# Fused trunk, MLP: scales behind the third product with tiles of their own, the first weight sums made ahead of the stage, two buffers for the values

## The chip, the cores and the metric

The kernel runs on one core of one Trainium2 chip. Its time is the device time of one execution in microseconds, the median of several runs. Below, the matrix engine is PE, the vector engine DVE, the scalar engine ACT, GpSimd POOL, and the engine that issues the transfers SP.

## The reference

Two layers over 1040 tokens (16 learned ones and 1024 given) of 1024 channels. Layer 0 mixes tokens with a short convolution and a gated delta rule, layer 1 with attention in a window. Each layer ends with an MLP whose gate goes through a causal convolution of width 3 along the tokens. All in float32. What the change touches is the MLP (w_up is 1024 x 5632, w_down 2816 x 1024):

```
for layer in range(DEPTH):
    hn = rms_norm(h, attn_norm_w[layer])
    ...
    h = h + mix.astype(h.dtype)
    ff = conv_ffn(rms_norm(h, ffn_norm_w[layer]), ffn_w_up[layer], ffn_conv_w[layer], ffn_w_down[layer])
    h = h + ff.astype(h.dtype)

def conv_ffn(h, w_up, conv_w, w_down):
    gate, val = jnp.split(h @ w_up, 2, -1)
    gate = causal_dwconv(gate, conv_w)
    return (jax.nn.silu(gate) * val) @ w_down
```

## The kernel before, in words

A float32 operand is kept as two rounded parts (tiles of the type that the profile calls fp32r), a high one and the low rest, and a product is three matmuls: high by high, high weights by low data, low weights by high data. High parts are made on ACT (a cast), low parts on DVE (a subtraction), in the stages' own weights at L134 and L135 (there on POOL or DVE), in the MLP at L814 and L815, for the MLP's data at L754 and L755.

The function ffn does an MLP. The tokens are cut in two halves of 520 columns (516 in layer 1), the channels into two halves of four tiles of 128. From these four blocks and the two halves of the weight columns it makes seven products instead of eight, in the manner of Strassen and Winograd: sums of data blocks on one side, sums of weight blocks on the other. The data side is made once for each MLP: X[0] to X[6], four tiles each, 28 tiles, with high and low parts. X[4] to X[6] are issued behind half_x, the last low part of X[3]. The weight side is made for each of the NF = 22 passes, each of 128 gate and 128 value columns.

A pass is seven products of 24 matmuls (L825), in this order: 0 into A (first, L842) and 1 into C, by the gate weights w1; 2 into A and 3 into C, by w2 (the sum sa = wv1 + wv2 - wg1 below and wv1 + wv2 above); 4 and 5 into A, by w3 (sb's first half, and wv2); 6 into C, by w4 (sb's second half). The first product of the next pass is put ahead of product 5. The buffers A and C are two banks each and rotate by two. ACT copies A out (p1, u2, u3); DVE adds to r (L871, L903) for the gate and to v (L894) for the values, multiplies the gate by the norm's factor (L904), does the convolution and the gate's nonlinearity (conv, L851 to L860), multiplies by v (L906), and SP writes the result to memory (fy, L907).

The norm's factor rstd isn't needed before L904, since it is taken out of the products. The function scales makes it from r, the sum of squares, which DVE adds up tile by tile (L741): four matmuls with ones (L761) for each half of tokens, and a short chain of ACT and DVE steps, in tiles th and sg which conv uses too.

Then comes the down projection: yf is read back from memory (L923), multiplied by rstd (L927), split into two parts (L928 on ACT, L929 on DVE), and multiplied by the down weights (gemm, L147), in five groups of passes (PARTS). Three loads of yf belong to the tail of the last pass, when PE still does its last products.

Tiles come from pools: fp is the MLP's own, wp is shared with the weights of the other stages (wo of the attention and the down weights too, through load_w). A tag in fp has one buffer if nothing else is said, in wp two; a writer waits for all readers of what was there before. In before, even passes load their weights into wp and odd ones into two buffers in fp; each third pair of high and low weight tiles is in fp, the others in wp. v has one buffer.

A scheduler sets the order of the instructions on each engine when the program is built, by the order in which the code issues them and when it thinks their operands are ready; a block under issue_after(x) comes behind x. That order is each engine's program. SP issues the transfers in its order too, and waits there for the buffers that they fill.

## Time and profile before

| what | value |
|---|---|
| median of 3 runs | 2385.93 us (2381.71 to 2390.98) |
| time of the profiled execution | 2385.68 us |
| its span | 2383.9 us |
| granted clock of PE, mean | 0.994 |
| PE busy | 2324.3 us, 98% |
| DVE busy | 1615.8 us, 68% |
| ACT busy | 973.4 us, 41% |
| POOL busy | 408.2 us, 17% |
| chain that ended last | PE 84%, DVE 10%, ACT 3% |

Times in rows are microseconds from the span's start. MLP 0 begins at about 583 and its passes end about 1041; MLP 1 begins at about 1668, when the attention's last product ends (1668.55), and its passes end about 2134. In a row of the timeline stand start, duration, engine, line, operation, result and operands, and the count; in square brackets the idle time of the engine before it and what ended that. Neighbouring rows of an engine can overlap by about 0.1 us, since an instruction begins while the one ahead drains: the step from one start to the next is the price of an instruction in a full queue.

### The profile page before, as it was taken

To read this page: it belongs to the slowest core of one execution; us is meant where nothing else is said; L and a number is where in the kernel's file an instruction comes from. 1 tells how busy PE (TensorE), PEld (TensorE's weight loads), DVE (VectorE), ACT (ScalarE), POOL (GpSimd) and SP (SyncE) were. 2 spreads that over 40 slices of the span, in tenths; PEclk is the share of its full clock that TensorE was granted. 3 is DMA by queue.
4 is the path that set the end of the run, shared out by engine and by line. 5 is a ranking of instruction groups with operands and counts; after the bars stand their busy time and mean duration, and the time that the engine had idled before them with its cause. 6 is when DMAs were issued, how large, how long until landed. Compare 5 with 4: busy or idle time off the path is not lost.

```text
span 2383.9 us, 39785 instructions
## 1 busy us (share of the span) xinstructions
PE 2324.3 (98%) x16000; PEld 2182.5 (92%) x16000; DVE 1615.8 (68%) x2799; ACT 973.4 (41%) x1952; POOL 408.2 (17%) x357
## 2 busy tenths in 40 slices
PE   8999999999999999999999999999899999999999
PEld 7989999999999999999999986778799999987887
DVE  8886745566877777777436466768977777778332
ACT  6544313434444444433116456656544444443110
POOL 1123323431000000012225233231000000002221
PEclk9999999999999999999999999999899999999999
DMA  4233534241222222154223110203222222234222
GB/s 139 79 128 121 170 111 138 76 161 72 89 81 81 81 76 76 63 188 139 66 60 129 45 36 19 89 27 116 81 89 81 81 81 77 72 142 169 76 67 102
DMA packets 93481, 224.83 MB, mean 94 GB/s; under 512 B 18672, under 2 KB 30264, under 8 KB 93296
## 3 DMA queue, kind: packets, MB, share of 16 engines
q1 hardware_dynamic: 93296, 222.28, 27.1%
q8 instruction: 126, 2.06, 0.3%
q14 instruction: 59, 0.48, 0.1%
HBM read 166.08 MB, written 56.15 MB: 93 GB/s over the span
## 4 chain that ended last, share of the span: by engine, by line
PE 84%; DVE 10%; ACT 3%; DMA 1%; issue 1%; POOL 0%; SPq 0%; ACTq 0%; DVEq 0%; POOLq 0%
PE mm L147 40%; PE A L825 20%; PE C L825 15%; PE scp L1067 1%; DVE qt L251 1%; PE po L1122 1%; DVE X L752 1%; PE qkp L971 1%; PE po L1125 1%; ACT xh L182 0%; DVE Xd L499 0%; DVE yl L171 0%; DVE fq L497 0%; DMA rb<-rq 0%; PE ptp L1096 0%
## 5 line engine op out<-in xcount | busy, mean ns | idle before, releaser
L825 PE MATMUL A<-X,whi 128*128 128x260 f32 (+1 forms) x2816 | 513.3, 283 | 5.6 <-ACT whi L814 3.2
L147 PE MATMUL mm<-y,wdh 128*128 128x346 f32 (+2 forms) x1760 | 471.0, 350 | 1.6 <-DVE r L903 1.6
L825 PEld LDWEIGHTS A<-X,whi 128*128 128x128 f32 x2816 | 434.0, 189 | 7.2 <-ACT whi L814 3.6
L825 PE MATMUL C<-X,whi 128*128 128x260 f32 (+1 forms) x2112 | 393.7, 285 | 7.8 <-DVE v L894 5.9
L825 PE MATMUL A<-X,wlo 128*128 128x260 f32 (+1 forms) x1408 | 392.6, 283 | 1.3 <-DVE wlo L815 1.3
L147 PEld LDWEIGHTS mm<-y,wdh 128*128 128x128 f32 x1760 | 315.1, 188 | 32.7 <-DVE r L903 2.0
L135 POOL TENSOR_TENSOR wdl<-wdr,wdh 128x512 fp32r<-128x512 f32 (+1 forms) x80 | 118.8, 1485 | 1311.7 <-ACT wdh L134 1302.4
L825 PEld LDWEIGHTS C<-X,whi 128*128 128x128 f32 x2112 | 330.7, 190 | 8.9 <-DVE v L894 6.3
L147 PE MATMUL mm<-y,wdl 128*128 128x346 f32 (+2 forms) x880 | 307.5, 350 | 0.6 <-POOL wdl L135 0.6
L825 PE MATMUL C<-X,wlo 128*128 128x260 f32 (+1 forms) x1056 | 297.5, 284 | 0.0
L825 PEld LDWEIGHTS A<-X,wlo 128*128 128x128 f32 x1408 | 264.2, 189 | 1.5 <-DVE wlo L815 1.5
L939 DVE TENSOR_TENSOR h<-mm,h 128x346 f32<-128x346 f32 (+2 forms) x200 | 115.9, 584 | 201.8 <-PE mm L147 201.0
L825 PEld LDWEIGHTS C<-X,wlo 128*128 128x128 f32 x1056 | 200.4, 190 | 0.0
L147 PEld LDWEIGHTS mm<-y,wdl 128*128 128x128 f32 x880 | 165.5, 188 | 16.8 <-POOL wdl L135 1.3
L815 DVE TENSOR_TENSOR wlo<-sa,whi 128x1024 fp32r<-128x1024 f32 x44 | 53.9, 1226 | 161.8 <-ACT whi L814 161.8
L134 ACT CAST wdh<-wdr 128x512 fp32r<-128x512 f32 (+1 forms) x80 | 53.1, 663 | 255.6 <-PE mm L147 221.9
L814 ACT CAST whi<-sb 128x512 fp32r<-128x512 f32 x88 | 54.7, 621 | 132.7 <-PE C L825 131.0
L147 PE MATMUL mm<-xl,wqkvh 128*128 128x346 f32 (+1 forms) x288 | 95.8, 333 | 1.4 <-DVE xl L183 1.4
L147 PE MATMUL mm<-xh,wqkvh 128*128 128x346 f32 (+1 forms) x288 | 96.3, 337 | 0.7 <-DVE row L269 0.7
L814 ACT CAST whi<-sa 128x1024 fp32r<-128x1024 f32 x44 | 46.1, 1048 | 115.7 <-PE A L825 115.0
L147 PE MATMUL mm<-xh,wqkvl 128*128 128x346 f32 (+1 forms) x288 | 93.0, 325 | 0.0
L928 ACT CAST y<-yf 128x346 fp32r<-128x346 f32 (+2 forms) x110 | 54.7, 536 | 93.1 <-DVE yf L927 73.7
(391 smaller groups left out, 5054.1 us busy)
## 6 DMA issues: line engine op xcount, KB each, us to landing
wg<-in_w_up SPq DMA_DIRECT2D x44, 512.0 KB, 3.2
wv<-in_w_up SPq DMA_DIRECT2D x44, 512.0 KB, 3.3
wdr<-in_w_down SPq DMA_DIRECT2D x48, 256.0 KB, 2.6
fy<-sg SPq DMA_DIRECT2D x22, 520.0 KB, 2.7
yf<-fy SPq DMA_DIRECT2D x22, 520.0 KB, 4.1
fy<-sg SPq DMA_DIRECT2D x22, 516.0 KB, 2.7
yf<-fy SPq DMA_DIRECT2D x22, 516.0 KB, 4.7
wdr<-in_w_down SPq DMA_DIRECT2D x32, 320.0 KB, 3.5
```

The lines of the kernel that those rows point to most:

```text
L134: ac.copy(hi, raw)
L135: eng.tensor_tensor(lo, raw, hi.bitcast(F32), ALU.subtract)
L147: pe.matmul(ps[:, :n], a[:, j, :], b[:, c0:c0 + n], start=(i == 0), stop=(i == last))
L251: ve.scalar_tensor_tensor(d, buf[:, pad + c0 - i:pad + c0 - i + n], taps[W - 1 - i], tmp[:, :n], ALU.mult, ALU.add)
L752: last_lo[:] = [ve.tensor_tensor(lo, src, hi.bitcast(F32), ALU.subtract).ins]
L814: ac.copy(hi, src)
L815: ve.tensor_tensor(lo, src, hi.bitcast(F32), ALU.subtract)
L825: pe.matmul(ps[:, b, :q], a[:, at + k, :], x[:, c], start=(start and n == 0), stop=(n == 11), skip_group_check=not start)
L928: ac.copy(yh[:, s], yf[:, s])
L939: ve.tensor_tensor(hn[m][:, s], ps[:, :n], hn[m][:, s], ALU.add)
L971: pe.matmul(p2[:, :n], ct[:, C_BD:C_BD + P], sq, start=True, stop=True)
L1067: pe.matmul(ps[:, :nk], qg[G][t][r, tok], kx[G][r, cols], start=True, stop=True)
```

## The change

Four things are changed, all in ffn; the arithmetic stays.

1. The scales are issued behind product 2 of pass 0, and no longer ahead of the passes. They take sg (half 0) or th (half 1) for their intermediate values, each half in its own, and the last step's tile t is rstd itself.
2. The weights of pass 0 are loaded, and its sums sa and sb and the two parts of sa made, ahead of the norm's squares (raws0, sa0, w20, sb0). For the other passes the same sums are made in the functions s21 and s34 as before.
3. v has two buffers. The temporaries t2 of the data side lie in these two (four halves), and no longer in two half tiles and v.
4. Which pool a tile comes from turns with the count of tiles: even passes now load into fp's two buffers, odd ones into wp, and of each three pairs of weight tiles the first is in fp.

```diff
@@ -724,9 +724,53 @@
                     def wide(tag):
                         return pu.tile([P, 2, 512], F32, tag=tag, name=tag)
 
-
                     def full(tag, bufs=1):
                         return fp.tile([P, 2 + 2 * hf], F32, tag=tag, name=tag, bufs=bufs)
+
+                    nw = [0]
+
+                    def wtile():
+                        nw[0] += 1
+                        p = fp if nw[0] % 3 == 1 else wp
+                        t = tuple(p.tile([P, KT, P], F32R, tag=tag, name=tag) for tag in ("whi", "wlo"))
+                        return t
+
+                    def wsplit(t, at, n, src):
+                        hi, lo = (x[:, at:at + n, :] for x in t)
+                        ac.copy(hi, src)
+                        ve.tensor_tensor(lo, src, hi.bitcast(F32), ALU.subtract)
+
+                    def weights(i):
+                        raws = []
+                        for n, at in (("wg", i), ("wv", NF + i)):
+                            r = (wp if i % 2 else fp).tile([P, KT, P], F32, tag="wraw", name=n, **({} if i % 2 else {"bufs": 2}))
+                            sp.dma_start(r, w_up[layer, at])
+                            raws.append(r)
+                        return raws
+
+                    def s21(raws):
+
+                        (wg, wv) = raws
+                        sa = fp.tile([P, KT, P], F32, tag="ws", name="sa", bufs=2)
+                        ve.tensor_tensor(sa[:, 4:8], wv[:, 0:4], wv[:, 4:8], ALU.add)
+                        ve.tensor_tensor(sa[:, 0:4], sa[:, 4:8], wg[:, 0:4], ALU.subtract)
+                        return sa
+
+                    def s34(raws, sa):
+
+                        (wg, wv) = raws
+                        sb = fp.tile([P, KT, P], F32, tag="ws", name="sb", bufs=2)
+                        ve.tensor_tensor(sb[:, 0:4], wg[:, 0:4], wv[:, 0:4], ALU.subtract)
+                        ve.tensor_tensor(sb[:, 4:8], sa[:, 0:4], wg[:, 4:8], ALU.subtract)
+                        return sb
+
+
+                    raws0 = weights(0)
+                    sa0 = s21(raws0)
+                    w20 = wtile()
+                    wsplit(w20, 0, KT, sa0)
+                    sb0 = s34(raws0, sa0)
+
 
                     sums = full("r", 2)
                     ss = [sums[:, s * hf:s * hf + hf] for s in range(2)]
@@ -759,15 +803,14 @@
                         ps = wide("C")
                         for b in range(2):
                             pe.matmul(ps[:, b, :q], ones, ss[s][:, b * q:b * q + q], start=True, stop=True)
-                        t = full("th")[:, :hf]
-                        ay = full("sg")
+                        ay, t = full("th" if s else "sg"), rstd[:, tk[s]]
                         a, y = ay[:, :hf], ay[:, hf:2 * hf]
                         ac.activation(two(a), ps[:, :, :q], AF.Identity, scale=1.0 / D, bias=epsc)
                         ac.activation(y, a.bitcast(I32), AF.Exp, scale=-0.5 * LN2 / (1 << 23), bias=seed)
                         for i, (sc, m3) in enumerate(((1.0, -3.00033), (0.25, -0.75))):
                             ac.activation(t, y, AF.Square, scale=sc)
                             ve.tensor_tensor(t, a, t, ALU.mult)
-                            ve.scalar_tensor_tensor(rstd[:, tk[s]] if i else y, t, m3, y, ALU.add, ALU.mult)
+                            ve.scalar_tensor_tensor(t if i else y, t, m3, y, ALU.add, ALU.mult)
 
                     w = [col(V_FN + 8 * layer + k) for k in range(KT)]
 
@@ -778,8 +821,8 @@
                         parts(1, k, B(1, k, 0), w[4 + k])
 
 
-                    vt2 = full("v")
-                    t2 = [half("t2", 2, "t2") if k < 2 else vt2[:, (k - 2) * hf:(k - 1) * hf] for k in range(4)]
+                    vt2 = [full("v", 2) for _ in range(2)]
+                    t2 = [vt2[k // 2][:, k % 2 * hf:(k % 2 + 1) * hf] for k in range(4)]
                     for k in range(4):
                         b11, b12, b21, b22 = B(0, k, 0), B(0, k, 1), B(1, k, 0), B(1, k, 1)
                         ac.activation(b12, b12, AF.Copy, scale=w[k])
@@ -790,8 +833,6 @@
                         parts(3, k, B(0, k, 0))
 
                     half_x = last_lo[0]
-                    for s in range(2):
-                        scales(s)
                     with tc.issue_after(half_x):
                         for k in range(4):
                             ve.scalar_tensor_tensor(B(0, k, 1), B(1, k, 1), w[4 + k], B(0, k, 1), ALU.mult, ALU.subtract)
@@ -800,19 +841,6 @@
                             ve.scalar_tensor_tensor(B(1, k, 0), B(1, k, 0), w[4 + k], t2[k], ALU.mult, ALU.subtract)
                             parts(5, k, B(1, k, 0))
                             parts(6, k, B(1, k, 1), w[4 + k])
-
-                    nw = [0]
-
-                    def wtile():
-                        nw[0] += 1
-                        p = fp if nw[0] % 3 == 0 else wp
-                        t = tuple(p.tile([P, KT, P], F32R, tag=tag, name=tag) for tag in ("whi", "wlo"))
-                        return t
-
-                    def wsplit(t, at, n, src):
-                        hi, lo = (x[:, at:at + n, :] for x in t)
-                        ac.copy(hi, src)
-                        ve.tensor_tensor(lo, src, hi.bitcast(F32), ALU.subtract)
 
                     def product(ps, wt, at, j, start):
                         hi, lo = wt
@@ -831,17 +859,9 @@
                         ac.copy(two(t), ps[:, :, :q])
                         return t
 
-                    def weights(i):
-                        raws = []
-                        for n, at in (("wg", i), ("wv", NF + i)):
-                            r = (fp if i % 2 else wp).tile([P, KT, P], F32, tag="wraw", name=n, **({"bufs": 2} if i % 2 else {}))
-                            sp.dma_start(r, w_up[layer, at])
-                            raws.append(r)
-                        return raws
-
                     def first(i):
 
-                        raws = weights(i)
+                        raws = weights(i) if i else raws0
                         w1 = wtile()
                         wsplit(w1, 0, KT, raws[0])
                         A = wide("A")
@@ -863,34 +883,35 @@
                     nxt = first(0)
                     for i in range(NF):
                         (wg, wv), w1, A, p1 = nxt
-                        g1, g2, v1, v2 = wg[:, 0:4], wg[:, 4:8], wv[:, 0:4], wv[:, 4:8]
+                        v2 = wv[:, 4:8]
                         Bk = wide("C")
                         product(Bk, w1, 4, 1, True)
                         r = full("r", 2)
                         ve.memset(r[:, 0:2], 0.0)
                         ve.tensor_tensor(two(r[:, 2:2 + hf]), Bk[:, :, :q], two(p1), ALU.add)
-
-                        sa = fp.tile([P, KT, P], F32, tag="ws", name="sa", bufs=2)
-                        w2 = wtile()
-                        with tc.issue_after(half_x) if i == 1 else nullcontext():
-                            ve.tensor_tensor(sa[:, 4:8], v1, v2, ALU.add)
-                            ve.tensor_tensor(sa[:, 0:4], sa[:, 4:8], g1, ALU.subtract)
-                            wsplit(w2, 0, KT, sa)
+                        if i == 0:
+                            sa, w2, sb = sa0, w20, sb0
+                        else:
+                            with tc.issue_after(half_x) if i == 1 else nullcontext():
+                                sa = s21((wg, wv))
+                                w2 = wtile()
+                                wsplit(w2, 0, KT, sa)
                         product(A, w2, 0, 2, False)
                         u2 = snap("u2", A)
+                        if i == 0:
+                            for s in range(2):
+                                scales(s)
                         C = wide("C")
                         product(C, w2, 4, 3, True)
-
-                        sb = fp.tile([P, KT, P], F32, tag="ws", name="sb", bufs=2)
                         w3 = wtile()
                         with tc.issue_after(half_x) if i < 2 else nullcontext():
-                            ve.tensor_tensor(sb[:, 0:4], g1, v1, ALU.subtract)
-                            ve.tensor_tensor(sb[:, 4:8], sa[:, 0:4], g2, ALU.subtract)
+                            if i:
+                                sb = s34((wg, wv), sa)
                             wsplit(w3, 0, 4, sb[:, 0:4])
                             wsplit(w3, 4, 4, v2)
                         product(A, w3, 0, 4, False)
                         u3 = snap("u3", A)
-                        v = full("v")
+                        v = full("v", 2)
                         ve.tensor_tensor(two(v[:, hf:2 * hf]), two(u3), C[:, :, :q], ALU.subtract)
                         if i + 1 < NF:
                             nxt = first(i + 1)
```

What the scheduler makes of it, at three places. First DVE in the tail of MLP 0's last pass, before:

```order
L927 TENSOR_TENSOR yf<-yf,rstd 128x348
L927 TENSOR_TENSOR yf<-yf,rstd 128x346 x2
L860 SCALAR_TENSOR_TENSOR sg<-th,sg 128x1040
L929 TENSOR_TENSOR y<-yf,y 128x348
L929 TENSOR_TENSOR y<-yf,y 128x346 x2
L906 TENSOR_TENSOR sg<-sg,v 128x1040
L894 TENSOR_TENSOR v<-u_10971,C 128x520
L903 TENSOR_TENSOR r<-u_10911,C 128x520
```

and after:

```order
L948 TENSOR_TENSOR yf<-yf,rstd 128x348
L948 TENSOR_TENSOR yf<-yf,rstd 128x346 x2
L915 TENSOR_TENSOR v<-u_10968,C 128x520
L880 SCALAR_TENSOR_TENSOR sg<-th,sg 128x1040
L950 TENSOR_TENSOR y<-yf,y 128x348
L950 TENSOR_TENSOR y<-yf,y 128x346 x2
L927 TENSOR_TENSOR sg<-sg,v 128x1040
L924 TENSOR_TENSOR r<-u_10908,C 128x520
```

The step that writes v (L894 before, L915 after; u is the copy u3, C the buffer of products) stood behind the multiplication by the old v (L906, now L927) and behind the low parts of y (L929, now L950); it now stands behind the steps on yf alone (L927, now L948). The order in MLP 1's tail is moved alike.

Second, SP at the same place, before:

```order
L131 DMA wdr<-in_w_down 128x512
L907 DMA fy_5957<-sg 128x1040
L923 DMA yf<-fy_5939 128x1040
L923 DMA yf<-fy_5940 128x1040
L923 DMA yf<-fy_5941 128x1040
L131 DMA wdr<-in_w_down 128x512
```

and after:

```order
L131 DMA wdr<-in_w_down 128x512
L928 DMA fy_5957<-sg 128x1040
L944 DMA yf<-fy_5939 128x1040
L944 DMA yf<-fy_5940 128x1040
L131 DMA wdr<-in_w_down 128x512
L944 DMA yf<-fy_5941 128x1040
L131 DMA wdr<-in_w_down 128x512
```

fy are the passes' results in memory, yf what the down projection reads of them, wdr the down weights, whose buffer in wp is one that the last pass's weights held. A load of down weights has moved ahead of the third load of yf.

Third, DVE at the end of the attention, ahead of MLP 1, before:

```order
L1188 TENSOR_TENSOR h_16829<-mm,h_16829 128x346
L741 TENSOR_TENSOR r<-r,sq 128x516
L1188 TENSOR_TENSOR h_16874<-mm,h_16874 128x334
L755 SCALAR_TENSOR_TENSOR X_17570<-h_16829,vt,X_17570 128x516
L755 SCALAR_TENSOR_TENSOR X_17573<-h_16116,vt,X_17573 128x516
L741 TENSOR_TENSOR r<-r,sq 128x516
L1188 TENSOR_TENSOR h_16874<-mm,h_16874 128x346
L135 TENSOR_TENSOR wol<-wor,woh 128x1024
```

and after:

```order
L755 TENSOR_TENSOR sa<-wv 128x512
L763 TENSOR_TENSOR sb<-wg,wv 128x512
L799 SCALAR_TENSOR_TENSOR X_17578<-h_16542,vt,X_17578 128x516
L785 TENSOR_TENSOR r<-r,sq 128x516
L1209 TENSOR_TENSOR h_16826<-mm,h_16826 128x334
L135 TENSOR_TENSOR wol<-wor,woh 128x1024
L756 TENSOR_TENSOR sa<-sa,wg 128x512
L799 SCALAR_TENSOR_TENSOR X_17590<-h_16587,vt,X_17590 128x516
L1209 TENSOR_TENSOR h_16826<-mm,h_16826 128x346
L785 TENSOR_TENSOR r<-r,sq 128x516
L764 TENSOR_TENSOR sb<-sa,wg 128x512
```

L1188 (now L1209) adds the attention's output products to h, L135 makes the low part of the output weights wo for one of these, L741 (now L785) adds squares, L755 (now L799) makes low parts of X. The two sums sa and sb of pass 0 (L755, L756, L763 and L764 after) now stand among these, and the low part of sa (L741 after) follows two rows further on; they stood behind the last of the L135 before. PE at this place had one half of the scales ahead of product 0 and the other behind it; now products 0 and 1 come first, and the scales' matmuls stand on both sides of the first matmuls of product 2.

## The prediction

> **What bounds the kernel now.** I read the page first, then PE's waits by what ended them, then windows over the passes and over the start of each MLP, then the single rows there. The page and the waits:
>
> ```profile
> span 2383.9 us, 39785 instructions
> PE 2324.3 (98%) x16000; PEld 2182.5 (92%) x16000; DVE 1615.8 (68%) x2799; ACT 973.4 (41%) x1952; POOL 408.2 (17%) x357
> ...
> engine line waited for: us in total, times, longest us
> PE C L761 <- DVE r L741: 8.9, 2, 7.9
> ...
> PE C L825 <- DVE v L894: 5.9, 2, 3.1
> ...
> PE A L825 <- ACT whi L814: 3.2, 2, 2.5
> ...
> PE C L825 <- DVE r L871: 1.4, 1, 1.4
> ```
>
> PE is busy for 2324.3 of 2383.9 us, so at most 59.6 us of its idle time can go. Three places that the diff touches hold 8.9 + 5.9 + 3.2 + 1.4 = 19.4 us of it: the matmuls of the scales (L761), product 6 behind the values (L894), and the first weights of each MLP. The windows (PE, PEld, DVE, ACT, POOL busy, PEclk, DMA share, GB/s), a steady stretch of passes first, then the start of MLP 0, then that of MLP 1:
>
> ```profile
> 650.00:670.00 20.00, 20.00 (x169) 20.00 (x168) 15.38 (x19) 8.55 (x12) 0.00 (x0) 1.00 0.22 80
> ...
> 585.00:595.00 10.00, 9.03 (x72) 8.70 (x71) 10.00 (x16) 8.37 (x15) 0.00 (x0) 1.00 0.14 56
> ...
> 1675.00:1680.00 5.00, 0.00 (x0) 0.00 (x0) 5.00 (x8) 3.91 (x8) 0.00 (x0) 0.50 0.00 0
> 1680.00:1685.00 5.00, 4.62 (x17) 4.25 (x18) 4.09 (x9) 4.28 (x8) 0.00 (x0) 0.50 0.00 0
> ```
>
> In the passes PE has no idle time and DVE works 15.38 of 20 us: an edit there gains nothing. At the starts it is the other way round: DVE is full and PE is the one with holes, at half clock behind the long one. So I take a start to be bounded by DVE's sum of work up to the last of the 28 X tiles, and a tail by the chain of DVE steps in front of product 6. That decides the forecast, because removing a wait of PE in front of a full DVE only moves the wait.
>
> **Start of MLP 1: -1.4 us.** The DVE rows that bound it, and PE's waits at both ends:
>
> ```profile
> 1666.51 1.23 DVE L815 TENSOR_TENSOR wlo<-wg,whi 128x1024 fp32r<-128x1024 f32 x1 [0.91 <-ACT whi L814]
> ...
> 1669.96 0.69 DVE L876 TENSOR_TENSOR sa<-wv 128x512 f32<-128x512 f32 x1
> 1670.56 0.75 DVE L787 SCALAR_TENSOR_TENSOR t<-h,vt,h 128x516 f32<-128x516 f32 x1
> ...
> 1682.51 0.69 DVE L770 SCALAR_TENSOR_TENSOR rstd<-th,sg 128x516 f32<-128x516 f32 x1 [0.91 <-DVE th L769]
> ...
> 1710.32 0.76 DVE L755 SCALAR_TENSOR_TENSOR X<-h,vt,X 128x516 fp32r<-128x516 f32 x1
> ...
> 1680.38 2.09 PE L761 MATMUL C<-r,ct 128*128 128x258 f32 x4 [7.93 <-DVE r L741]
> ...
> 1711.13 0.38 PE L825 MATMUL C<-X,whi 128*128 128x258 f32 x1 [0.53 <-DVE X L755]
> ```
>
> PE's last wait of the start is for X: product 6 of pass 0 begins its last k at 1711.13, behind DVE's step at 1710.32; from there PE is full. From the norm's first residual sum to that X step, DVE has 108 instructions in both orders, the same ones, only in another sequence. Their sum doesn't change, so the end can move only by DVE's idle time in between. That is 0.91 us at 1666.51 (the low part of pass 0's first weights waits for ACT's high part, and that for the weights' load) and 0.91 at 1682.51 (the scales' chain waits for its own last step): 1.8 us. The first goes since pass 0's weights now lie in the pool that is free early and their loads are issued first; the second goes since the scales stand later, among other work. What comes in is DVE waiting for the attention's output products: the moved weight sums stand in front of three of the low parts of wo (L135), for which those products wait. They are five steps, four of 128x512 at 0.60 (1669.96 to 1670.56) and one of 128x1024 at 1.14 (its duration of 1.23 less the 0.09 by which the row at 1669.96 overlaps the next), 3.55 us. PE will stall there for part of it; DVE has other work meanwhile. The trace has no such wait; the nearest rows are the two of 0.91, so I bound DVE's new idle time by 0 and 0.9 and take the middle, 0.4, since the steps in front are work that DVE must do anyway. -1.8 + 0.4 = -1.4, between -0.9 and -1.8. The 8.9 us in front of the scales vanish from the view of waits, and come back as waits for wo and X.
>
> **Start of MLP 0: -1.4 us.**
>
> ```profile
> 580.16 0.52 DVE L699 TENSOR_TENSOR h<-mm,h 128x346 f32<-128x346 f32 x1 [2.63 <-PE mm L147]
> ...
> 586.80 1.22 DVE L815 TENSOR_TENSOR wlo<-sa,whi 128x1024 fp32r<-128x1024 f32 x1
> ...
> 597.57 0.69 DVE L888 TENSOR_TENSOR sb<-sa,wg 128x512 f32<-128x512 f32 x1
> ...
> 614.08 0.77 DVE L755 SCALAR_TENSOR_TENSOR X<-h,vt,X 128x520 fp32r<-128x520 f32 x1
> ```
>
> Here DVE idles before 580 (2.63 us at 580.16) and is full from there on. The change puts the low part of the second weights (586.80, 1.14 us) and the two halves of sb (0.60 each; the second is the row at 597.57) into the idle stretch: -2.35 us. Two steps of the scales, now later in the order, fall in front of the last X step instead of behind it: 2 x 0.60 = +1.2. The last X step so ends 1.15 us earlier. Of what PE has left at that point, two matmuls fewer (0.12 us each) remain: -0.24. Sum -1.4; bounds -0.5 (X steps held by ACT's high parts) and -1.7. That PE now waits less at 598 (the 2.5 us of the view) gains nothing more, by the same reasoning.
>
> **The two tails: -3.2 and -4.4 us.** MLP 0's last pass, DVE, then PE; then MLP 1's:
>
> ```profile
> 1032.32 1.36 DVE L927 TENSOR_TENSOR yf<-yf,rstd 128x348 f32<-128x348 f32 x3
> 1033.61 1.23 DVE L860 SCALAR_TENSOR_TENSOR sg<-th,sg 128x1040 f32<-128x1040 f32 x1
> 1034.76 1.36 DVE L929 TENSOR_TENSOR y<-yf,y 128x348 fp32r<-128x348 f32 x3
> 1036.05 1.23 DVE L906 TENSOR_TENSOR sg<-sg,v 128x1040 f32<-128x1040 f32 x1
> 1037.38 0.70 DVE L894 TENSOR_TENSOR v<-u,C 128x520 f32<-128x520 f32 x1
> 1041.30 0.70 DVE L903 TENSOR_TENSOR r<-u,C 128x520 f32<-128x520 f32 x1 [3.22 <-PE C L825]
> ...
> 1034.74 0.28 PE L825 MATMUL A<-X,wlo 128*128 128x260 f32 x1
> 1038.13 0.51 PE L825 MATMUL C<-X,whi 128*128 128x260 f32 x2 [3.12 <-DVE v L894]
> ...
> 2128.75 0.69 DVE L894 TENSOR_TENSOR v<-u,C 128x516 f32<-128x516 f32 x1
> 2133.92 0.69 DVE L903 TENSOR_TENSOR r<-u,C 128x516 f32<-128x516 f32 x1 [4.48 <-PE C L825]
> ...
> 2126.46 0.28 PE L825 MATMUL A<-X,wlo 128*128 128x258 f32 x1
> 2129.49 0.80 PE L825 MATMUL C<-X,whi 128*128 128x258 f32 x2 [2.75 <-DVE v L894]
> ```
>
> Product 6 accumulates into C, which L894 must have read; L894 writes v, of which there is one buffer, so it stands behind the multiplication that reads the old v (L906). With two buffers it stands behind the yf steps alone: it can start at 1033.61 and end at 1034.31, before product 5's last matmul ends (1034.74 + 0.28 = 1035.02). So the 3.12 us go and product 6, 24 matmuls at 0.12 = 2.87 us, ends at 1037.9. Then DVE is next: the same five steps fill it to 1037.38 + 0.70 = 1038.08, so L903's step moves from 1041.30 to 1038.08: -3.2. MLP 1: product 5 ends at 2126.74, product 6 then at 2129.5 to 2129.6, DVE is free at 2129.45; L903's step moves from 2133.92 to 2129.55: -4.4. This is more than its wait of 2.75, since behind the wait the matmuls run slow (0.80 for two against 0.51 in MLP 0). Everything behind L903 (the down projection, full on PE) shifts with it.
>
> The Trainium skill (TensorE: Matmul & The Clock Gate, Part 1, The HAM clock gate) says that the clock falls to half after an idle window of about 3.4 us. By that rule alone a wait of 2.75 us would cost no clock, MLP 1's tail would give 2.9, and the sum would be 1.5 smaller; the rows show slow matmuls behind 2.75 us and nearly full ones behind 3.12, so the rows decide (the page's free-running window leaves room for this).
>
> **Sum.** -1.4 - 1.4 - 3.2 - 4.4 = -10.4 us. The profiled execution took 2385.68 us, of which the span is 2383.9; it becomes 2375.3. The median of the three runs, 2385.93, is 0.25 above it, so I forecast 2375.5. A measurement of this kernel tells about 0.5%, 11.9 us, from no change: the sum stays just within. If every term reaches its upper bound it is -1.7 - 1.8 - 3.2 - 4.4 = -11.1, still within.
>
> **Rivals.**
> 1. PE's waits are the limit after all: all 19.4 us of them go, with the half clock behind them (half of the 4.62 busy us in 1680 to 1685, 2.3, and the 1.5 of MLP 1's tail): up to 23.2 us. Against it: DVE's full windows. For it: PE may find other products ready in the new sequence, so that less is left behind the last X step. At 19.4 to 23.2 us: 2362.7 to 2366.5; it shares out down to 11.9 us, 1.5 more than my sum. Chance 0.27, half of it above 2367.
> 2. The tails don't come, because L894's place isn't what holds it, but the copy of u3 or the buffer C: only the starts, 2385.9 - 2.8 = 2383.1. Against it: DVE runs without a gap from 1032.32 to 1038.08, so its order does hold it. Chance 0.10, partial losses included.
> 3. Slower: the tail's third load of yf. In SP's order a load of down weights, which must wait until the last pass's gate and value weights are used (the low part of wv, DVE L815), now stands in front of it:
>
> ```profile
> 1015.45 7.50 SPq L923 DMA_DIRECT2D yf<-fy  x3
> 1025.67 0.69 DVE L815 TENSOR_TENSOR wlo<-wv,whi 128x512 fp32r<-128x512 f32 x1
> ...
> DMA to landing us min/median/max: 4.3/7.8/11.2
> ...
> yf<-fy SPq DMA_DIRECT2D x22, 520.0 KB, 4.1
> ```
>
> Before, the three were issued by 1022.9; now the third goes out at about 1026.6 (1025.67 + 0.69 and the issue). At the median of 4.1 it lands at 1030.7, in time for DVE's yf step at 1032.32. But the v step now stands behind that yf step, and the three steps behind it (1.15, 1.29, 1.33 by the starts above) in front of L903's. From a landing of 5.7 each us counts, from 9.0 MLP 0's tail gains nothing. The row with min, median and max is of the weights' loads (L838) between 470 and 620; at their longest, 11.2, yf lands at 1037.8, v is done at 1039.8, DVE is full to 1043.5, and L903's step is 2.2 late instead of 3.2 early. With 2.1 for MLP 1, worked out likewise, -2.8 + 4.3 = +1.5: 2387.4, slower than before from a landing of 10.4 on. Chance 0.03, since yf's own median is 4.1. The Trainium skill (DMA: Bandwidth & Descriptors, Issuing engines are not separate DMA queues) has transfers interleave on the same 16 engines whoever starts them; by that the weights in front would lengthen this landing. No run here shows the two together.
> 4. A wait in each pass: the tiles of high and low parts change places among the pools, and their ring could come round too early.
>
> ```profile
> 796.83 1.22 DVE L815 TENSOR_TENSOR wlo<-sa,whi 128x1024 fp32r<-128x1024 f32 x1 [4.03 <-ACT whi L814]
> ...
> 800.88 0.40 PE L825 MATMUL A<-X,whi 128*128 128x260 f32 x2
> ```
>
> The low part of a pass's second weights is done at 798.05, product 2 uses it from 800.88: 2.8 us to spare. It decides when a reused tile comes free 2.8 us later than now; a wait of 0.27 us in 44 passes would make 11.9, 2397.8. The ring has three pairs of tiles in the same rotation in both, so 0.04.
> 5. The second buffer isn't given and the sequence stays: the order shows the v step moved, so 0.01.
>
> My forecast has 0.55. Faster by over 0.5%: 0.27 (rival 1). Within: 0.55 + 0.10 + 0.03 + 0.01 = 0.69. Slower: 0.04 (rival 4). A range of 2367 to 2384 holds the forecast, rival 2 and half of rival 1: about 0.8.
>
> **What would show it.** Right: no wait of PE for v at either tail, L147 beginning 3.2 and 4.4 us sooner after product 5; the wait for the scales' sums gone, but waits for X of similar length in the 40 us after the attention; DVE full up to the last X step, which comes 1 to 2 us earlier. Wrong: DVE idle for over 2 us between 1642 and 1710, PE waiting for yf or wol for more than 3 us, or holes on PE in the steady passes.

## The result and the profile after

The changed kernel takes 2374.07 us (median of 6 runs, 2370.27 to 2378.61) where the kernel before takes 2387.45 (6 runs of the same session, 2381.71 to 2390.98): a ratio of 0.9946, with a 95% interval of 0.993 to 0.9962. That is 13.4 us less; the forecast was 10.4 less. The profiled execution has a span of 2368.5 us, 15.4 less than before.

From the page of the profile after, and from its view of PE's waits:

```profile
span 2368.5 us, 39717 instructions
PE 2320.9 (98%) x16000; PEld 2179.6 (92%) x16000; DVE 1607.0 (68%) x2799; ACT 973.2 (41%) x1952; POOL 412.8 (17%) x357
...
PE A L853 <- ACT u L859: 3.1, 4, 1.6
PE A L853 <- ACT p L859: 3.0, 1, 3.0
PE mm L147 <- DVE h L1209: 3.0, 4, 1.1
PE A L853 <- ACT whi L740: 2.8, 2, 1.9
...
PE A L853 <- DVE X L796: 2.3, 2, 1.7
```

The waits for r in front of the scales (8.9 us) and for v (5.9) are gone. In MLP 1's start, waits for ACT's copy p (3.0 us), for weights (whi, 2.8) and for X (2.3) stand in place of the one of 7.9 for r: PE idles 8.2 us there, before 10.8. At the end of the attention waits for h are new (3.0 us). The long hole in the windows of MLP 1's start has become several short ones (PE, PEld, DVE, ACT, POOL busy, PEclk, DMA share, GB/s; the same work comes about 10 us earlier than in the rows of before):

```profile
1665.00:1670.00 5.00, 3.27 (x24) 2.80 (x23) 4.17 (x7) 3.11 (x6) 0.00 (x0) 1.00 0.44 175
1670.00:1675.00 5.00, 3.71 (x16) 3.53 (x17) 4.96 (x9) 4.33 (x8) 0.00 (x0) 0.66 0.00 0
1675.00:1680.00 5.00, 4.65 (x40) 4.44 (x38) 5.00 (x9) 5.00 (x11) 0.00 (x0) 1.00 0.00 0
1680.00:1685.00 5.00, 1.37 (x7) 0.96 (x7) 5.00 (x10) 2.77 (x5) 0.00 (x0) 0.96 0.32 105
1685.00:1690.00 5.00, 4.74 (x22) 4.74 (x23) 5.00 (x9) 1.88 (x4) 0.00 (x0) 0.50 0.01 3
```

MLP 0's tail on the timeline after, DVE and then PE:

```profile
1026.34 1.37 DVE L948 TENSOR_TENSOR yf<-yf,rstd 128x348 f32<-128x348 f32 x3
1027.63 0.68 DVE L915 TENSOR_TENSOR v<-u,C 128x520 f32<-128x520 f32 x1
1028.24 1.23 DVE L880 SCALAR_TENSOR_TENSOR sg<-th,sg 128x1040 f32<-128x1040 f32 x1
...
1032.92 0.68 DVE L924 TENSOR_TENSOR r<-u,C 128x520 f32<-128x520 f32 x1
...
1028.74 0.29 PE L853 MATMUL A<-X,wlo 128*128 128x260 f32 x1
1028.86 0.41 PE L853 MATMUL C<-X,whi 128*128 128x260 f32 x2
...
1031.73 0.48 PE L147 MATMUL mm<-y,wdh 128*128 128x348 f32 x2
```

Product 6 follows product 5 at the next step (1028.74, 1028.86), because v is done at 1028.3. And the down projection begins at 1031.73, ahead of the r step at 1032.92: before, it began 0.75 us behind the start of that step.

To see where the time came from, I cut each execution at the same PE instructions: mixer (of which the stretch from its 941st to its 976th matmul, at 170 to 180 us, is shown alone), MLP start (from the last L147 matmul in front to the 481st matmul of the products), MLP tail (from the 3601st of these to the first L147 matmul of the down projection), and the attention's end (the last 260 matmuls or so of L147). Differences to the first profile of before, in us, from the starts of these instructions in each trace:

| stretch | after | after, again | before, again | second buffer alone | scales alone | sums alone |
|---|---|---|---|---|---|---|
| mixer, 170 to 180 | -3.8 | -2.4 | 0.0 | -0.2 | 0.0 | 0.0 |
| MLP 0 start | -1.0 | -1.0 | +1.2 | +0.2 | +1.8 | +0.8 |
| MLP 0 tail | -4.3 | -4.3 | +1.5 | -3.3 | +1.4 | -0.9 |
| attention's end | +3.4 | +3.5 | +0.2 | -0.2 | -0.2 | +3.4 |
| MLP 1 start | -2.8 | -3.8 | -0.2 | +0.6 | 0.0 | -3.6 |
| MLP 1 tail | -5.3 | -5.3 | +0.1 | -4.3 | +0.1 | +0.1 |
| whole span | -15.4 | -12.6 | +3.5 | -7.0 | +2.2 | +5.7 |

| stretch | all but second buffer | all but scales | all but sums | sums behind wo | squares on POOL | squares left out |
|---|---|---|---|---|---|---|
| mixer, 170 to 180 | 0.0 | -0.2 | 0.0 | -3.2 | -3.8 | 0.0 |
| MLP 0 start | +0.6 | +0.9 | +2.6 | +0.6 | +2.0 | +0.4 |
| MLP 0 tail | +0.6 | -2.4 | -4.3 | -4.3 | -4.3 | -4.3 |
| attention's end | +3.4 | +3.4 | -0.2 | +2.2 | +8.8 | +2.2 |
| MLP 1 start | -3.9 | -2.8 | +1.0 | -3.4 | -2.5 | -4.9 |
| MLP 1 tail | -2.3 | -4.3 | -5.2 | -5.3 | -5.3 | -5.3 |
| whole span | -2.6 | -5.9 | -8.7 | -14.4 | -3.1 | -10.8 |

The passes take the same time to 0.3 us in all. The rest of a span (the down projections, the other parts of mixer and attention) differs by up to 3.1 us in a stretch from the first profile of before, and by up to 1.2 us between the two of before.

### The profile page after: what moved, and what is told of

It is laid out like the page before. It is cut to its first block, busy times and chain, and to the rows that moved or that the text cites. A ratio compares the mean times of both kernels' runs of the same rounds, so it can differ in the third digit from the quotient of the medians.

```text
span 2368.5 us, 39717 instructions
## 1 busy us (share of the span) xinstructions
PE 2320.9 (98%) x16000; PEld 2179.6 (92%) x16000; DVE 1607.0 (68%) x2799; ACT 973.2 (41%) x1952; POOL 412.8 (17%) x357
## 4 chain that ended last, share of the span: by engine, by line
PE 85%; DVE 9%; ACT 3%; DMA 2%; issue 1%; POOL 1%; SPq 0%; ACTq 0%; DVEq 0%; POOLq 0%
PE mm L147 40%; PE A L853 21%; PE C L853 16%; PE scp L1088 1%; DVE qt L251 1%; PE po L1143 1%; DVE fq L497 1%; PE qkp L992 1%; DVE yl L171 1%; PE po L1146 0%; DMA fh<-h 0%; PE ptp L1117 0%; DVE Xd L499 0%; ACT xh L182 0%; DMA rb<-rq 0%
## 5 line engine op out<-in xcount | busy, mean ns | idle before, releaser
L147 PE MATMUL mm<-y,wdh 128*128 128x346 f32 (+2 forms) x1760 | 471.8, 350 | 0.0
L135 POOL TENSOR_TENSOR wdl<-wdr,wdh 128x512 fp32r<-128x512 f32 (+1 forms) x80 | 121.9, 1524 | 1298.2 <-ACT wdh L134 1293.8
L147 PEld LDWEIGHTS mm<-y,wdh 128*128 128x128 f32 x1760 | 315.2, 188 | 31.2
L147 PE MATMUL mm<-y,wdl 128*128 128x346 f32 (+2 forms) x880 | 308.0, 350 | 0.0
L147 PEld LDWEIGHTS mm<-y,wdl 128*128 128x128 f32 x880 | 165.4, 188 | 15.8 <-POOL wdl L135 0.2
L741 DVE TENSOR_TENSOR wlo<-sa,whi 128x1024 fp32r<-128x1024 f32 x44 | 53.9, 1225 | 177.0 <-ACT whi L740 177.0
L147 PE MATMUL mm<-xl,wqkvh 128*128 128x346 f32 (+1 forms) x288 | 95.2, 331 | 1.5 <-DVE xl L183 1.5
L147 PE MATMUL mm<-xh,wqkvh 128*128 128x346 f32 (+1 forms) x288 | 95.6, 335 | 0.7 <-DVE row L269 0.7
L147 PE MATMUL mm<-xh,wqkvl 128*128 128x346 f32 (+1 forms) x288 | 92.4, 322 | 0.0
L859 ACT COPY u<-A 128x520 f32<-128x520 f32 (+1 forms) x88 | 52.1, 592 | 95.6 <-PE A L853 95.6
```

The costliest lines, as they stand in the source:

```text
L135: eng.tensor_tensor(lo, raw, hi.bitcast(F32), ALU.subtract)
L147: pe.matmul(ps[:, :n], a[:, j, :], b[:, c0:c0 + n], start=(i == 0), stop=(i == last))
L741: ve.tensor_tensor(lo, src, hi.bitcast(F32), ALU.subtract)
L859: ac.copy(two(t), ps[:, :, :q])
```

## The experiments

My theory after the result: the tails carry the change, through the second buffer and through an earlier down projection; the starts give nothing, because DVE's sum of work bounds them; the mixer's 3.8 us are chance. The rival: PE's waits at the starts were the cost, and their removal is the gain.

**The second buffer alone.** The kernel before with two edits:

```diff
-vt2 = full("v")
-t2 = [half("t2", 2, "t2") if k < 2 else vt2[:, (k - 2) * hf:(k - 1) * hf] for k in range(4)]
+vt2 = [full("v", 2) for _ in range(2)]
+t2 = [vt2[k // 2][:, k % 2 * hf:(k % 2 + 1) * hf] for k in range(4)]
...
-v = full("v")
+v = full("v", 2)
```

> The kernel before with nothing but the values' second buffer (and the temporaries t2 in the two). Theory (tails carry the gain): in both tails the wait for v goes, the down projection begins 3.2 us sooner in MLP 0 and 4.4 us in MLP 1, but still waits for the r step (0.8 us each), since the scales are placed as before; the starts stay within 0.5 us. Sum -7.6, a time ratio of about 0.997. Rival (the starts carry the change's gain, through PE's waits there): no more than 2 us.

Measured: 2378.63 us (5 runs) against 2387.67, ratio 0.9961 (0.9947 to 0.9975). The tails give -3.3 and -4.3, as expected to a tenth, and in each the first product of the down projection still waits. Its timeline, PE in MLP 0's tail:

```profile
1037.07 0.28 PE L825 MATMUL C<-X,wlo 128*128 128x260 f32 x1
1038.14 0.59 PE L147 MATMUL mm<-y,wdh 128*128 128x348 f32 x2 [0.79 <-DVE r L903]
```

This one edit holds most of what the whole change gains.

**The scales alone.** The kernel before with the calls moved behind product 2 and the tiles of the diff's scales:

```diff
-for s in range(2):
-    scales(s)
...
 u2 = snap("u2", A)
+if i == 0:
+    for s in range(2):
+        scales(s)
```

> The kernel before with nothing but the scales behind the third product and their own tiles. Theory (DVE's sum of work bounds the starts): PE's wait of 7.9 us in front of the scales goes from the view, but comes back in front of weights and X tiles; the passes of MLP 1 run at most 1.5 us sooner, those of MLP 0 at most 1 us; the tails gain 0.9 us each because the down projection's first product no longer waits for the r step. Sum -2 to -4. Rival (PE's waits are the limit): -8 us or more at MLP 1's start, ratio 0.996.

Measured: 2386.7 us (11 runs), ratio 0.999 (0.998 to 0.9999). The wait of 7.9 us is gone, and MLP 1's start is where it was (0.0): PE's idle time there is 10.1 us, before 10.8, only now in front of weights and of v. The rival, -8, falls. The tails didn't give the 0.9 each. The wait for r is gone, but product 6 ran at half speed throughout, behind the same wait for v. In MLP 0's tail, the start of that product, its last matmul, and DVE's r step, which waits for its end:

```profile
1040.03 0.80 PE L822 MATMUL C<-X,whi 128*128 128x260 f32 x2 [3.12 <-DVE v L894]
...
1045.18 0.42 PE L822 MATMUL C<-X,wlo 128*128 128x260 f32 x1
...
1045.63 0.70 DVE L903 TENSOR_TENSOR r<-u,C 128x520 f32<-128x520 f32 x1 [5.66 <-PE C L822]
```

The same 24 matmuls took 3.2 us in the first profile of before (1038.13 to 1041.30), 5.6 here.

**The sums alone.** The changed kernel without the second buffer and with the scales as before; pass 0's weights, sums and parts ahead of the stage, and the turn of the pools, are left:

```diff
+raws0 = weights(0)
+sa0 = s21(raws0)
+w20 = wtile()
+wsplit(w20, 0, KT, sa0)
+sb0 = s34(raws0, sa0)
```

> The kernel before with nothing but pass 0's weights, their sums and parts ahead of the stage (and the turn of the pools that goes with it). Theory: at MLP 1 the attention's last product ends about 3 us later, because the weight sums stand in front of the attention's last output steps on DVE; the start makes up for that, and the passes run within 1 us of before; in MLP 0 they run 1 us sooner. Sum -1, ratio 0.9995. Rival (PE's waits are the limit): the waits of 3.2, 1.4 and 1.3 us for weights and r go, -5 us.

Measured: 2388.82 us (11 runs), ratio 1.0008 (0.9999 to 1.0017). The attention ends 3.4 us later, MLP 1's start takes 3.6 less, as expected. MLP 0's start came out 0.8 longer, not 1 shorter. (The turn of the pools was run with the sums only, never alone.)

**All but the second buffer**, the changed kernel with the two edits of the first experiment undone.

> The whole change without the values' second buffer. Theory: the tails keep their waits for v (3.1 and 2.8 us); the down projection no longer waits for the r step, -0.9 us in each; the two starts together within 1 us of before. Sum -2 to -3 us against before, ratio 0.999, beside whatever the first layer's mixer does by chance. Rival (starts carry it): -5 us or more from the starts.

Measured: 2385.63 us (11 runs), ratio 0.9993 (0.9984 to 1.0002). The starts and the attention's end give +0.6 + 3.4 - 3.9 = +0.1 together: without the second buffer nothing is left that the runs can tell from no change. The tails differ from what I expected (+0.6 and -2.3) by the speed of product 6 again.

**All but the scales**, the changed kernel with the second experiment's edit undone.

> The changed kernel with the scales in their old place and old tiles. Theory: the tails gain -3.3 and -4.3 us, 1 us less in each than the changed kernel, because the down projection's first product waits for the r step again (0.8 us); the starts within 1.5 us of before. Sum -7 to -9. Rival (the scales' place has nothing to do with that wait): tails as in the changed kernel.

Measured: 2380.19 us (7 runs), ratio 0.9971 (0.996 to 0.9982). The waits for r are back, 1.8 us in MLP 0's tail and 0.8 in MLP 1's, and the tails give -2.4 and -4.3. So the scales' edit decides that wait, not the second buffer: in the eight profiles that have it the wait never comes. Without it the wait comes in nine of ten tails; the one without is MLP 0's with the sums alone, so the rest of the order has a say in it too.

**All but the sums**: the first and second experiment's edits together, in the kernel before.

> The kernel before with the scales behind the third product and the second buffer for the values, but pass 0's weight sums in their old place. Theory: the tails gain all of the change (-4.3 and -5.3 us), since neither waits for v nor for the r step; the starts stay within 1.5 us of before, as in the runs of the scales alone; the attention's end isn't delayed. Sum -8 to -10 us, ratio 0.996, within 2 us of the changed kernel beside the mixer. Rival (the weight sums are worth something when the scales are gone too): 3 us or more behind the changed kernel at the starts.

Measured: 2378.22 us (5 runs), ratio 0.9961 (0.9948 to 0.9973). The tails are those of the changed kernel (-4.3, -5.2). But the starts lose: +2.6 in MLP 0, +1.0 - 0.2 in MLP 1, 3.4 us together where the changed kernel has -1.0 + 3.4 - 2.8 = -0.3. My expectation failed here and the rival held in this profile: once the scales stand behind product 2, the sums made ahead pay 3.7 us, above all in MLP 0's start, where the last X step comes 34.1 us behind the mixer's last product without them and 29.5 with them. How much of the 3.7 belongs to the kernel is open. Half clock lasts 10.2 us in MLP 0's start here and 3.4 in the changed kernel, 17.1 against 10.2 in MLP 1's, and that differs from one execution to the next. PE's waits in MLP 0's start without the sums made ahead:

```profile
594.96 0.74 PE L822 MATMUL C<-X,whi 128*128 128x260 f32 x2 [2.20 <-ACT th L764]
608.72 0.51 PE L822 MATMUL A<-X,whi 128*128 128x260 f32 x2 [0.68 <-ACT u L828]
613.01 0.59 PE L822 MATMUL A<-X,whi 128*128 128x260 f32 x1 [2.83 <-DVE X L752]
```

**The sums behind wo.** The changed kernel, with the four lines that make sa0, w20 and sb0 run in MLP 0 only; in MLP 1 pass 0 makes its sums in its turn, as the other passes do.

```diff
-sa0 = s21(raws0)
+if layer == 0:
+    sa0 = s21(raws0)
...
-if i == 0:
+if i == 0 and layer == 0:
     sa, w2, sb = sa0, w20, sb0
...
-if i:
+if i or layer:
     sb = s34((wg, wv), sa)
```

> The changed kernel, but in MLP 1 pass 0's sums, and their two parts, are issued in their old place; the loads stay ahead. Theory (DVE's sum of work bounds the start): the attention's last product comes 3.4 us sooner again, and the start of MLP 1 gives that back but for 1 us; the passes of MLP 1 run within 1 us of the changed kernel. Rival (the delayed attention costs what it shows): -3.4 us, ratio to before 0.993.

Measured: 2374.95 us (5 runs), ratio 0.9947 (0.9934 to 0.9959), the same as the changed kernel. The attention ends 1.2 us sooner, not 3.4, since 1.8 us of PE's waits for h are left. MLP 1's passes begin 1.8 us sooner than in the first profile of the changed kernel and 0.9 sooner than in its second; MLP 0's start, whose code is the same, 1.5 later. So none of the 1.2 us was given back in MLP 1, against my expectation, and the rival's 3.4 us didn't come either; the whole time is the same. That a later end of the attention is made up in the start was shown by the sums alone (3.4 later, then 3.6 less).

**Squares left out and squares on POOL.** Two tests of whether DVE's sum of work bounds the starts. In one, 12 of the 14 additions are left out; in the other all 14 go to POOL:

```diff
-ve.tensor_tensor(ss[s], ss[s], sq, ALU.add)
+if j < 2: ve.tensor_tensor(ss[s], ss[s], sq, ALU.add)
```

```diff
-ve.tensor_tensor(ss[s], ss[s], sq, ALU.add)
+gp.tensor_tensor(ss[s], ss[s], sq, ALU.add)
```

> The changed kernel with 12 of the 14 additions of squares of each MLP left out and put nowhere (the norm's factor then lacks six of eight channel tiles), 7.3 us less work on DVE at each start. Theory (DVE's sum bounds the starts): the last X step and the passes of MLP 1 come 5 to 7 us sooner, MLP 0's 2 to 5 us. Rival (PE's waits bound): under 1.5 us in each.

> The changed kernel with the 14 additions of squares of each MLP on POOL, which is idle there, instead of DVE (0.6 us each there, 8.5 us in all). Theory (DVE's sum of work bounds the starts): the last X step of MLP 1 comes 4 to 8 us sooner and the passes run 4 to 7 us sooner; MLP 0 gains 2 to 5 us. Span 2358 to 2364, ratio to before 0.990. Rival (PE's own waits bound it, DVE's fullness is only work pulled forward): within 1.5 us of the changed kernel. If POOL's additions slow DVE's instructions by more than they take off, slower.

Measured with the additions left out (one run, 2375.01 us), in MLP 1: 2.2 - 4.9 = -2.7 where the changed kernel has +0.7 and, in its second profile, -0.3. So 7.3 us less work on DVE brought 2.4 to 3.4 us. The rest became idle time of DVE: from the start of the attention's end to the last X step it idles 14.6 us, in the changed kernel 10.0, most of the difference in front of ACT's steps and PE's products. DVE's sum has a part in the bound, but isn't all of it; that ACT's and PE's own chains lie close behind is my reading, and no run takes them apart. In MLP 0 it brought nothing (+0.4 against -1.0): there the additions stand beside the mixer's last products, where DVE idles anyway. My expectation for MLP 0 overlooked that.

On POOL: 2382.56 us (11 runs), ratio 0.9981 (0.9972 to 0.9989), 8 us slower than the changed kernel. The attention's end takes 8.8 us more than before. DVE there, and one of POOL's additions in the same stretch:

```profile
1645.28 1.77 DVE L799 SCALAR_TENSOR_TENSOR X<-h,vt,X 128x516 fp32r<-128x516 f32 x1
1647.39 2.23 DVE L135 TENSOR_TENSOR wol<-wor,woh 128x1024 fp32r<-128x1024 f32 x1
...
1657.03 1.21 DVE L135 TENSOR_TENSOR wol<-wor,woh 128x1024 fp32r<-128x1024 f32 x1
...
1647.24 1.29 POOL L785 TENSOR_TENSOR r<-r,sq 128x516 f32<-128x516 f32 x1 [0.74 <-ACT sq L784]
```

The same DVE instruction takes 2.23 us where it begins behind an addition on POOL, and 1.21 without one: such an addition costs DVE about 1 us where it saves it 0.6. From the start of the attention's end to the last X step DVE is busy for 81.9 us, in the changed kernel for 81.6, although the 14 additions have left it. The Trainium skill (Perfetto Trace Analysis, Optimizing Scalar/DVE Operations) says that moving work between these two might not help, since they share a read port of SBUF; these rows agree, with a loss.

**The changed kernel again, and the kernel before again.**

> The changed kernel once more, for the stages that the change doesn't touch. Theory: the 3.8 us that its first profile gained in the first layer's mixer at 170 to 180 us (the wait for qk of 0.8 instead of 3.1) belong to that execution: a second profile shows about 3.1 again, span about 2372. Rival (they come with the change, by where its tiles lie): 0.8 again, span about 2368.5. The tails and starts as in the first profile, within 0.5 us.

> The kernel before once more, for the first layer's mixer at 170 to 180 us and for the clock in the tails. Theory (the mixer's 3.8 us and the clock behind a wait of 3 us are matters of one execution): the stretch at 170 to 180 us may come out up to 3.8 us shorter than in the first profile, and product 6 behind the waits for v takes anything from 2.9 to 5.6 us. Rival (both belong to the kernel): as in the first profile within 0.3 us, 3.2 and 4.4 us.

Measured: the changed kernel 2374.44 us (4 runs), ratio 0.9953 (0.9938 to 0.9968); span 2371.3. The mixer's stretch gave -2.4, between the two expectations. The kernel before gave 0.0 there, as in its first profile, and product 6 took 4.7 us in MLP 0's tail where the first profile had 3.2, at the same wait of 3.1.

```profile
1043.75 0.70 DVE L903 TENSOR_TENSOR r<-u,C 128x520 f32<-128x520 f32 x1 [4.72 <-PE C L825]
...
600.00:605.00 5.00, 5.00 (x23) 5.00 (x24) 5.00 (x8) 2.47 (x4) 0.00 (x0) 0.50 0.41 155
```

The second row is its window in MLP 0's start: a clock of 0.50 where the first profile has 0.68, with the same waits in front. Half clock lasts 6.8 us there instead of 3.4, which fits the 1.2 us by which that start is longer. So a start's length is known to 1 or 2 us from one profile, and so is that of a tail with a wait for v.

The mixer's stretch hangs on one step, which PE waits for. DVE in before, then after, and POOL in before, then after:

```profile
173.22 2.71 DVE L307 SCALAR_TENSOR_TENSOR qk<-qk,rb 128x1040 f32<-128x1040 f32 x1 [0.59 <-DMA rb<-rq]
```

```profile
171.78 1.24 DVE L307 SCALAR_TENSOR_TENSOR qk<-qk,rb 128x1040 f32<-128x1040 f32 x1 [0.38 <-DMA rb<-rq]
```

```profile
172.40 2.43 POOL L135 TENSOR_TENSOR wgil<-wgir,wgih 128x1024 fp32r<-128x1024 f32 x1 [6.58 <-ACT wgih L134]
```

```profile
171.94 3.32 POOL L135 TENSOR_TENSOR wgil<-wgir,wgih 128x1024 fp32r<-128x1024 f32 x1 [6.60 <-ACT wgih L134]
```

Where the load of rb lands late, the step begins behind POOL's subtraction and takes 2.71 us instead of 1.24. In after it begins 0.16 us ahead of the subtraction, and it is the subtraction that gets longer, 3.32 us against 2.43. In all thirteen profiles the one of the two that began first kept its time (1.24 on DVE, 2.3 to 2.4 on POOL) and the other took longer (2.4 to 3.2, and 3.3 to 3.4). DVE's step came first in four of the five profiles of kernels with all three parts of the change, and in none of the eight without. The instructions of the mixer are the same in all. If the change had nothing to do with it, such a split would come about once in 140 times; so it probably comes with the change, but the runs don't show how.

## Why the forecast was near, point by point

The forecast was -10.4 us for the profiled execution. The stretches from MLP 0 on sum to -10.6, and the mixer's -4.8 (3.8 in the one stretch), which the forecast left out, make the -15.4. The medians say -13.4. The sum was near partly because two errors cancelled: MLP 1's start gave 2.1 us less than its term, the tails 2.0 more. And that the time forecast, 2375.5 us, is within 1.5 us of the measured one is luck too: with three more runs the median of before moved from 2385.93 to 2387.45.

- **What bounds the starts.** Half right. The reading that a wait of PE in front of a full DVE only moves held: taking away the 7.9 us alone changed MLP 1's start by 0.0, and from the start of the attention's end to the last X step PE idled 9.9 to 11.6 us in each of the eleven profiles with all squares on DVE, whatever it waited for. That DVE's sum of work up to the last X step is the bound was too simple. 7.3 us less of that work brought 2.4 to 3.4. And with the second buffer, the scales or the sums alone that step came 1.6 to 2.1 us sooner behind the start of the attention's end, while the 481st matmul of MLP 1's products moved by 0.4 us at most against the same point. What does bound the start is open.
- **MLP 1's start, -1.4.** Wrong; measured +0.7 (3.4 - 2.8), in the second profile -0.3. The step that failed is "I bound DVE's new idle time by 0 and 0.9 and take the middle". From 1642 to 1710, and in the same 68 us of the changed kernel's profiles, DVE idles 1.96 us before and 1.41 and 1.35 after. The two old waits of 0.91, for weights and for the scales, went, but 1.1 us came in front of ACT's product of h (L828), not in front of the attention's products. Against the start of the attention's end the last X step came 0.0 and 0.2 us sooner, not 1.4. And PE lost 3.0 us, more than a part of 3.55, in front of the additions of h (L1209) which stand behind the moved sums and set the output banks free:

```profile
1647.48 0.42 PE L147 MATMUL mm<-yh,woh 128*128 128x346 f32 x1 [1.07 <-DVE h L1209]
...
1669.19 0.75 DVE L829 SCALAR_TENSOR_TENSOR h<-h,vt 128x516 f32<-128x516 f32 x1 [0.68 <-ACT h L828]
```

- **MLP 0's start, -1.4.** The size was about right: -1.0 in both profiles, within its bounds. The terms on DVE were right too. Behind the mixer's last product the last X step comes 2.15 us sooner with the sums alone (worked out: 2.35), moving the scales too gives 1.2 of that back (worked out: 1.2), and in the changed kernel it is 0.9 sooner. But that step doesn't set the start's length: the sums alone made the start 0.8 longer, since PE had 328 matmuls left from the step to the 481st, instead of 302, and behind the step PE never idled there in any of the thirteen profiles. What differs is PE's idle time and half clock in front of it. The kernel with the sums behind wo, whose code and X step are the same in MLP 0, came out at +0.6, and before's second profile at +1.2. So the nearness of -1.0 to -1.4 is in part luck.
- **The tails, -3.2 and -4.4.** The mechanism was right, the second buffer alone gave -3.3 and -4.3. The whole gave -4.3 and -5.3, 1 us more in each. The step that failed is "Then DVE is next ... so L903's step moves from 1041.30 to 1038.08", by which the down projection went on waiting for the r step. With the scales behind the third product it doesn't: the first product of the down projection begins ahead of this step (1031.73 against 1032.92), so it gets a buffer that the step doesn't hold.
- **The half clock as a term of MLP 1's tail** (1.5 of the 4.4). It isn't a property of that tail. Behind a wait of 2.7 to 3.1 us, in the ten tails of five profiles, product 6 took 3.2 us three times, 4.4 to 4.7 five times and 5.6 twice; without a wait it took 2.9 (1028.86 to 1031.73). The granted clock in the traces shows what decides: it changes only at the ends of windows of 3.41 us, which lie elsewhere in each execution, and in these tails half clock lasts one or two of them. In the seven tails with half clock PE idled 2.1 to 3.1 us of the window ahead of it; in the other three the wait was split over two windows, with 1.7 us or less in each. In the first profile of before, the two windows of MLP 0's wait, then that of MLP 1's and the next (PE busy, PEclk, DMA share, GB/s):

```profile
1033.24:1036.66 3.42, 1.78 (x15) 1.00 1.01 353
1036.66:1040.07 3.41, 1.94 (x16) 1.00 0.98 386
2125.51:2128.92 3.41, 1.23 (x11) 1.00 0.97 364
2128.92:2132.34 3.42, 2.85 (x13) 0.50 1.02 383
```

The Trainium skill (TensorE: Matmul & The Clock Gate, Part 1, The HAM clock gate) puts the fall to half behind an idle window of about 3.4 us that runs free of the kernel. The traces agree on the length and on the free running; but a window that was idle for 2.1 us of its 3.41 was enough here. (Elsewhere in the thirteen traces 1.2 us was enough in one window, and 1.9 wasn't in another, so no exact share shows.) The 1.5 us were right for the profile that the forecast was read from, by how its windows happened to lie.
- **Rival 3** (the third load of yf behind the down weights). The load went out late, as worked out (the changed kernel's SP):

```profile
1009.18 7.07 SPq L944 DMA_DIRECT2D yf<-fy  x2
1020.41 0.33 SPq L131 DMA_DIRECT2D wdr<-in_w_down  x1
1020.85 0.37 SPq L944 DMA_DIRECT2D yf<-fy  x1
...
DMA to landing us min/median/max: 3.5/3.5/3.5
```

It landed after 3.5 us, at 1024.4, 1.9 us ahead of the yf step at 1026.34. The slack worked out in the prediction was of that size, and held.
- **Rival 1** (all of PE's waits go) fell with the scales alone, **rival 2** with the second buffer alone, **rival 4** with the passes, which take the same time to 0.3 us in every kernel.

## What to carry to other kernels

A wait on the busiest engine is worth what the engines behind it can give: before counting it, look whether the engine that ends it is full over the whole stretch, and expect the wait to move if it is. A buffer that an in-order engine must write before it has finished with the old value costs most at the end of a loop, where no next pass fills the hole; there one more buffer was worth 7.6 us in the profile, and the rest of the change only a little more. Compare the last and the first stage of a loop apart from its steady part, and profile the same kernel twice before believing a difference of a microsecond or two in them: how the clock's windows lie to the waits is another matter in each execution.

## What the runs showed that I had not expected

- An addition on POOL of 1.3 to 1.4 us lengthens a DVE instruction that begins behind it by about 1 us (2.23 against 1.21, 1.77 against 0.75 as in the rows of before), so that work moved there cost more than it took off. Of a DVE step and a POOL subtraction that overlap, the one that begins second pays.
- A wait of about 3 us on PE costs anything from 0.3 to 2.7 us of half clock behind it, in the same kernel and place (3.2 and 4.7 us for the same 24 matmuls in two profiles of before), by how it lies to windows of 3.41 us.
- Three edits that alone give 0.9961, 0.999 and 1.0008 give 0.9946 (0.9953 the second time) together: the order is made anew from all of them. Beside the second buffer, the scales' edit took the wait for r out of the tails, and the mixer's gain came only with all three.
